# One-hots of the expert gates: 16-bit operands on VectorE, tokens innermost, eight at a step, in a hybrid decoder step

## The chip, the cores and the metric

The kernel runs on one core of a Trainium2 chip. The metric is the device time of one execution in microseconds (us). Before the change three runs took 4259.34, 4259.7 and 4266.0 us; the median is 4259.7. Lines (L974) are lines of the kernel before.

## The reference

One layer of a decoder trunk on 544 tokens (512 of a prompt, 8 sequences of 4 sampled ones), width 2048, everything in float32. A recurrence branch and a sliding-window attention branch are merged by sigmoid gates; then comes a product-key expert mixer (PEER), then a per-layer input embedding. The change is in the mixer:

```python
q = (xt @ w_q).reshape(n, PEER_HEADS, 2, D_KEY // 2)          # 8 heads, two halves of 128
s = jnp.einsum('nhpd,hpkd->nhpk', q, sub_keys)                # 128 keys each
s1, i1 = lax.top_k(s[:, :, 0], 16); s2, i2 = lax.top_k(s[:, :, 1], 16)
cand = s1[..., :, None] + s2[..., None, :]; cidx = i1[..., :, None] * 128 + i2[..., None, :]
top_s, sel = lax.top_k(cand.reshape(n, 8, 256), 16)           # 16 picks a head
idx = jnp.take_along_axis(cidx.reshape(n, 8, 256), sel, axis=-1); g = jax.nn.softmax(top_s, axis=-1)
hb = jax.nn.gelu(jnp.einsum('chkd,cd->chk', u[idx], x))       # 16384 experts
out = jnp.einsum('chk,chkd->cd', hb * g, v[idx])
```

So every token has 128 picks (8 heads by 16), each a pair of key indices (a, b), which name expert 128 a + b, and a gate.

## The kernel before, in words

**Dense and fetched tokens.** The first 416 tokens (`DC`) meet all 16384 experts in two dense products: H = gelu(U x) in 128 output tiles, then V^T (H * G), where G holds each token's gates at its experts and zero elsewhere. The last 128 tokens fetch their experts' rows of U and V one by one with indirect DMAs that GpSimd issues (L1039). A fetched row of U is multiplied with the tokens on VectorE (L1046); a fetched row of V is scaled on ScalarE (L1052) and added up on GpSimd (L1053).

**The weight pipeline.** All products run through `run_units`. A unit is a half chunk of 8 tiles of 128x128 weights. SyncE loads it (`wr`, L217), ScalarE rounds it to the high half (`wh`, L224), VectorE subtracts to get the low half (`wl`, L225), three buffers each, and the split of a unit is issued two units ahead. Every weight tile then makes three matmuls (high by high, high by low, low by high). In the products with U and V these are matmuls of 416 columns at L280, 24 a unit. An output tile of U is two units; VectorE scales its sum (L1092), ScalarE applies gelu (L1093) and issues the write to DRAM (L1094).

**The order of the side work.** Everything else that belongs beside the products is written as generators. Each `yield` names a cost in us of VectorE (0.5 where it names none). `side()` is called twice a unit, after four matmuls and at the unit's end. It adds a credit (1.256 in the product with U), takes off what a use of a fetched U row costs (2.3), and runs steps (`advance`) until the credit is used. So the order of instructions on every engine's queue is fixed when the program is built; only the waits are decided at run time. Before the 24th unit from the end of U (`gates_done`), all steps that are still open are run at once.

**The gates.** The generators run one after another. For each tile of 128 tokens (the last has 32) `tk1` and `tk2` find the picks on VectorE (top 16, index arithmetic) and bring them to `pt`, one pick on each partition and the tokens along the row: a, b and gate. Then G is made. For each token, a one-hot of a (128 picks by 128 keys) and a one-hot of b times the gate, multiplied on TensorE, give the 128x128 square of gates of that token. The gate stands as a sum of two float16 numbers (a high and a low part, `gh`), so each square is two matmuls that add up.

- L997 and L999 make, for four tokens, the one-hots `ob` and `oa` on VectorE: `iota` (float32) is compared with b or a (float32), with a float16 output, keys innermost, 128x512 elements.
- L1001 multiplies the one-hot of b with the low and the high part of the gates on GpSimd, twice 128x512.
- `place` (L974) takes the oldest of up to `QB` = 4 held groups: 8 matmuls of 128 columns into a PSUM tile `aux` (two buffers, of which one half is used). One step later ScalarE copies it to `gst` (L976) with the tokens innermost, so that it writes every 128 bytes.
- After 32 tokens (`TC`) ScalarE issues the write of `gst` (one buffer, 2 MB) to `Gd` in DRAM (L978). The product with V reads it back later.

The 416 tokens make 104 groups of four, 832 matmuls and 13 writes.

Of the kernel before, what the change touches and what calls it, by code (L numbers as in the profile page):

```python
# [9 lines left out]
F32 = mybir.dt.float32  # L10
# [7 lines left out]
P = 128  # L18
D = 2048
KT = D // P  # L20
NP = 512            # prompt tokens
NB, ND = 8, 4       # sample batch, tokens per sequence
T = NP + NB * ND    # token columns: prompt, then (b, t)
HB = T // 2
LP = 568            # columns of the recurrence layout: prompt, 3 spare, then (b, 7)
LH = LP // 2
RN = 8              # recurrence tiles
EPS = 1e-6
NEG = -1e30
NS = P              # last token columns, whose experts' rows are fetched one by one  # L30
DC = T - NS         # token columns that meet all experts in dense products
TC = 32             # tokens per chunk of the gate scratch
NCH = DC // TC
NW = 24             # operand pairs of the second PEER product
QB = 4
# [7 lines left out]
NWA = 2 * KT * T // (2 * DC)    # of these, the pairs that lie in the activations' space  # L43


def _token_tiles(t0, t1):
    """Tiles of nt tokens with ng head groups on the partitions: row = group * nt + token."""
    out = []
    while t0 < t1:
        nt = next(n for n in (128, 64, 32) if n <= t1 - t0)  # L50
        out.append((t0, nt, P // nt))
        t0 += nt
    return out
# [13 lines left out]
def _build(ctx, tc, nc, I, O):  # L67
# [47 lines left out]
    # sum of squares of the raw columns, folded to 1/rms of every column on every partition  # L115
    ssum = {}

    def sq_add(k, pool, x=0):
        """x: whose sum it joins, VectorE's or GpSimd's (which squares for itself)"""
        new = x not in ssum  # L120
        if new:
            ssum[x] = misc[:, (4 + x) * T:(5 + x) * T]
        s = ssum[x] if new else pool.tile([P, T], F32, name="sq", tag=f"sq{x}", bufs=2 - x)
        if x:
            GP.tensor_mul(s, raw[:, k, :], raw[:, k, :])
        else:
            A.activation(s, raw[:, k, :], AF.Square)
        if not new:
            (GP if x else V).tensor_add(ssum[x], ssum[x], s)
# [18 lines left out]
    def side():  # L148
        """A part of the work beside the products: steps worth pace["main"] us of the vector engine."""
        SPS["tick"] = SPS.get("tick", 0) + 1  # L150
        owed["sp"] += pace["sp"]
        if owed["sp"] >= 1:
            owed["sp"] -= 1
            owed["main"] -= sp_step()
        owed["main"] = min(owed["main"] + pace["main"], 2 * pace["main"])
        while owed["main"] > 0:
            c, more = advance()
            owed["main"] -= c
            if not more:
                break  # L160
# [4 lines left out]
    def unit(src, groups, **kw):  # L165
        """src: [128, 8, 128]; groups: (accumulator key, [(kl, operand getter)], start, stop, epilogue)"""
        units.append(dict(src=src, groups=groups, **kw))

    def gemm(src, ops, epi, nk=2, cols=None, **kw):
        """One output tile: nk half chunks of 8 k tiles, operands ops(k)."""  # L170
# [8 lines left out]
    def advance():  # L179
        cost, more = 0.0, bool(active or gens)  # L180
        while len(active) < maxact[0] and gens:
            if gens[0] is None:      # what follows needs everything before it
# [148 lines left out]
    # RG-LRU branch  # L331
# [10 lines left out]
    def decay_rate():  # L342
        # sp4 = 4 * softplus(-lam), with log1p kept accurate for small arguments
# [97 lines left out]
    # attention branch  # L441
# [208 lines left out]
    def start_ple():  # L650
        for k in range(2):
            t = pL.tile([P, T], F32, name="pin", tag="pin", bufs=2)
            SP.dma_start(out=t, in_=I["pT"][k])
            h, l = act_tile(KT - 2 + k)      # free until the last operands of w_in are split
# [95 lines left out]
    NGB = 3             # buffers of fetched rows  # L750
# [27 lines left out]
    def post_out():  # L778
# [4 lines left out]
        U_["iota"] = aconst(pU, "iota", [P, P])  # L783
# [3 lines left out]
    def rs_and_x():  # L787
        yield from make_rs(rs2)
        xg = U_["p"].tile([P, KT, NS], F32, name="xg", tag="gst", bufs=1)
# [37 lines left out]
    def scores(q):  # L827
        pU = U_["p"]
        kt = pU.tile([P, 4, P], F32, name="skl", tag="eq", bufs=1)
        SP.dma_start(out=kt, in_=I["skT"][:, q * 4:q * 4 + 4, :])  # L830
        for ti, (t0, nt, ng) in enumerate(TT):
# [7 lines left out]
            st = pU.tile([P, 512], F32, name="scst", tag="scst", bufs=2)  # L839
# [13 lines left out]
    def tk1(ti, q):  # L853
# [5 lines left out]
        sc = pU.tile([P, 4, P], F32, name="scp", tag="scp", bufs=2)  # L859
# [11 lines left out]
        # pairs (a, b) of ranks with (a + 1)(b + 1) <= 16 hold the 16 best: a = 0, then 1..7 with b < 8,  # L871
        # then 8..15 with b = 0, in the order of the flat index
# [13 lines left out]
    def tk2(ti):  # L886
# [5 lines left out]
        # ranks (a, b) of every pick, from its place among the pairs  # L892
# [18 lines left out]
        # the chosen key pair of every pick  # L911
        for x in range(2):
            for h2 in range(0, nh, 2):
# [3 lines left out]
                eq = pU.tile([P, 2, 16, 16], F32, name="eq", tag="eq", bufs=1)  # L917
                V.tensor_tensor(out=eq[:, :w], in0=U_["iota"][:, None, None, 0:16].to_broadcast(sh),
# [7 lines left out]
        # gates  # L926
# [20 lines left out]
        for x in range(3):  # L947
# [3 lines left out]
            # rows (group, token) to rows (group, pick): every group's picks in columns of its own  # L951
            ex = pU.tile([P, ng, n], F32, name="ex", tag="ex", bufs=2)
# [9 lines left out]
        # a gate, times GS to keep it in float16's range, as the sum of two float16  # L962
        g16 = pU.tile([P, P], F16, name="g16", tag="mk", bufs=1)
        gh = pU.tile([P, 2, P], F32, name="gh", tag="hu", bufs=1)
        A.activation(g16[:, :nt], pt[:, 2, :nt], AF.Copy, scale=GS)
        A.activation(gh[:, 0, :nt], g16[:, :nt], AF.Copy)
        yield
        V.scalar_tensor_tensor(gh[:, 1, :nt], pt[:, 2, :nt], GS, gh[:, 0, :nt], op0=ALU.mult, op1=ALU.subtract)
        def place(c0, gst, q0, oa, ob):
            ps = psum.tile([P, 2, 512], F32, name="aux", tag="aux", bufs=2)  # L970
            pq = ps[:, 0, :].rearrange("p (q i) -> p q i", i=P)
            for q in range(4):
                for x in range(2):
                    PE.matmul(pq[:, q], lhsT=oa[:, q, :], rhs=ob[:, q, x, :], start=x == 0, stop=x == 1)  # L974
            yield
            A.activation(gst[:, :, q0:q0 + 4].rearrange("p i q -> p q i"), pq, AF.Copy, scale=1.0 / GS)  # L976
            if q0 == TC - 4:
# [5 lines left out]
        def place_next():  # L983
            c0, q0, oa, ob = held.popleft()
# [4 lines left out]
            yield from place(c0, gst[0], q0, oa, ob)  # L989

        for c0 in range(0, nt, TC):
            for q0 in range(0, TC, 4):
                oa = pU.tile([P, 4, P], F16, name="oa", tag="oa", bufs=QB)
                ob = pU.tile([P, 4, 2, P], F16, name="ob", tag="ob", bufs=QB)
                tk = slice(c0 + q0, c0 + q0 + 4)
                io = U_["iota"][:, None, :].to_broadcast([P, 4, P])
                V.tensor_tensor(out=ob[:, :, 0, :], in0=io, in1=pt[:, 1, tk, None].to_broadcast([P, 4, P]),  # L997
                                op=ALU.is_equal)
                V.tensor_tensor(out=oa, in0=io, in1=pt[:, 0, tk, None].to_broadcast([P, 4, P]), op=ALU.is_equal)  # L999
                for x in (1, 0):  # L1000
                    GP.tensor_tensor(out=ob[:, :, x, :], in0=ob[:, :, 0, :],  # L1001
                                     in1=gh[:, x, tk, None].to_broadcast([P, 4, P]), op=ALU.mult)
                yield 1.2
                held.append((c0, q0, oa, ob))
# [6 lines left out]
    # the fetched experts: one pick of every row of a sparse tile at a time, the rows of U against the  # L1011
    # tokens on the vector engine, those of V, a batch later, into the sums on GpSimd
# [136 lines left out]
    def wfirst():  # L1149
        """Products for the first group; the operands that fit beside U's."""  # L1150
# [18 lines left out]
    def wsecond():  # L1169
        """In place of the first half of U's operands."""  # L1170
# [32 lines left out]
    def weave(n=3):  # L1203
        """The first halves of the last n tiles, then the second halves."""
# [34 lines left out]
    # operands of the last product go where the last group's W leave room, in the order that they leave  # L1239
# [28 lines left out]
    def post_first(g, lo, hi):  # L1268
        """The first halves of the last tiles are through: their operands' place is free."""
# [179 lines left out]
```

## Time and profile before

| | |
|---|---|
| median of three runs | 4259.7 us |
| profiled execution, span | 4266.4 us |
| TensorE (PE) busy | 4122.2 us, 97% |
| weight loads (PEld) busy | 4024.8 us, 94% |
| VectorE (DVE) busy | 2807.7 us, 66% |
| ScalarE (ACT) busy | 1534.6 us, 36% |
| GpSimd (POOL) busy | 1224.6 us, 29% |
| product with U, about | 1520 to 2900 us |
| product with V, about | 2900 to 4040 us |

The profiled execution is one execution recorded by the hardware, and its own time is the span: 4266.4 us from the first to the last record, 6.7 us above the median of the runs. Busy time is the union of an engine's instructions. [...] A view of waits names, for an engine's line, the instruction whose end it waited for. A view of stretches gives the busy time of each engine within given bounds. Views by form keep groups of instructions of the same shapes apart, with busy time, the mean of one in ns, and the engine's idle time before them with what ended it.

### The profile page before, as it was taken

Reading aid. Unit: us, or ns where it says so; the run is one execution under the profiler, and the core shown is the slowest. Engines: PE = TensorE matmul, PEld = TensorE weight load, DVE = VectorE, ACT = ScalarE, POOL = GpSimd, SP = SyncE. Lnnn points to the kernel's source line nnn. Section 1 sums busy time; section 2 is a strip of 40 time slices with the busy share of each in tenths; the row PEclk is TensorE's granted clock in tenths of the full one; section 3 lists DMA queues with packets and bytes.
Section 4 is the critical chain, followed back from the end, with each engine's and each line's share of the span. In section 5 each row is a group of like instructions: output and inputs, shape, how many; then the busy total and the mean of one; then the engine's idle time right before and its main releaser. Section 6 shows DMA issues by size and latency. Waiting matters only on the chain.

```text
span 4266.4 us, 63247 instructions
## 1 busy us (share of the span) xinstructions
PE 4122.2 (97%) x26089; PEld 4024.8 (94%) x26089; DVE 2807.7 (66%) x3659; ACT 1534.6 (36%) x1799; POOL 1224.6 (29%) x723
## 2 busy tenths in 40 slices
PE   7999999999999999999888988889999999999999
PEld 7999999999999999999878988889999999999999
DVE  7755444233434369888887988757888878877443
ACT  4442334321223233343343344334444444332331
POOL 3000000000000001464485377413555555410000
PEclk9999999999999999999999999999999999999999
DMA  5232232243343347677666666668989888997333
GB/s 180 80 125 79 75 106 86 84 135 134 124 131 104 111 144 266 234 274 254 215 231 213 233 209 217 224 221 289 332 312 332 326 315 314 323 327 248 118 131 102
DMA packets 323154, 848.69 MB, mean 199 GB/s; under 512 B 26409, under 2 KB 170729, under 8 KB 290097
## 3 DMA queue, kind: packets, MB, share of 16 engines
q1 hardware_dynamic: 204960, 492.69, 34.3%
q0 software_dynamic: 44864, 295.20, 18.6%
q10 hardware_dynamic: 73040, 56.76, 4.0%
q8 instruction: 204, 3.34, 0.3%
q14 instruction: 86, 0.70, 0.0%
HBM read 760.78 MB, written 83.77 MB: 198 GB/s over the span
## 4 chain that ended last, share of the span: by engine, by line
PE 85%; DVE 9%; ACT 2%; issue 2%; DMA 1%; ACTq 1%; POOL 0%; SPq 0%; DVEq 0%
PE acc L280 45%; PE acc L284 36%; DVE wl L225 4%; DVE raw L1046 1%; PE aux L974 1%; ACTq L1094 1%; ACT wh L224 1%; DVE misc L1092 1%; PE aux L519 1%; ACT gst L976 1%; PE aux L556 1%; DMA Gd<-gst 0%; PE aux L284 0%; ACT misc L1093 0%; PE aux L836 0%
## 5 line engine op out<-in xcount | busy, mean ns | idle before, releaser
L225 DVE TENSOR_TENSOR wl<-wr,wh 128x1024 fp32r<-128x1024 f32 x764 | 1220.6, 1599 | 1291.3 <-ACT wh L224 1287.7
L280 PE MATMUL acc<-opf,wh 128*128 128x416 f32 x7424 | 2038.5, 356 | 0.9 <-ACT wh L224 0.9
L280 PEld LDWEIGHTS acc<-opf,wh 128*128 128x128 f32 x7424 | 1405.4, 191 | 16.5 <-ACT wh L224 1.8
L224 ACT ACTIVATE wh<-wr 128x1024 fp32r<-128x1024 f32 x764 | 805.0, 1058 | 1577.9 <-PE acc L284 801.3
L284 PE MATMUL acc<-opf,wh 128*128 128x272 f32 x7936 | 1348.9, 292 | 22.3 <-ACT wh L224 9.1
L280 PE MATMUL acc<-opf,wl 128*128 128x416 f32 x3712 | 1316.5, 355 | 52.1 <-DVE wl L225 52.0
L284 PEld LDWEIGHTS acc<-opf,wh 128*128 128x128 f32 x7936 | 1140.7, 190 | 36.0 <-issue 15.1
L284 PE MATMUL acc<-opf,wl 128*128 128x272 f32 x3968 | 827.7, 290 | 0.0
L280 PEld LDWEIGHTS acc<-opf,wl 128*128 128x128 f32 x3712 | 708.8, 191 | 68.4 <-DVE wl L225 62.8
L284 PEld LDWEIGHTS acc<-opf,wl 128*128 128x128 f32 x3968 | 628.5, 189 | 0.3 <-DVE wl L225 0.3
L1001 POOL TENSOR_TENSOR ob<-ob,gh 128x512 f16<-128x512 f16 x208 | 313.1, 1510 | 71.2 <-DVE ob L997 60.1
L1053 POOL TENSOR_TENSOR raw<-raw,gb 128x2048 f32<-128x2048 f32 x59 | 276.8, 4692 | 124.2 <-ACT gb L1052 123.9
L1093 ACT ACTIVATE misc<-misc 128x416 f32<-128x416 f32 x128 | 70.6, 552 | 573.1 <-DVE misc L1092 573.1
L1039 POOL DMA_INDIRECT gb<-i_vn,idx x91 | 115.9, 1274 | 384.2 <-DVE gb L1046 222.5
L1053 POOL TENSOR_TENSOR raw<-raw 128x2048 f32<-128x2048 f32 x37 | 177.8, 4805 | 161.6 <-ACT raw L1052 161.6
L280 PE MATMUL acc<-wx,wh 128*128 128x416 f32 x768 | 206.8, 350 | 0.0
L1046 DVE SCALAR_TENSOR_TENSOR raw<-raw,misc 128x2048 f32<-128x2048 f32 x69 | 172.8, 2504 | 0.0
L1039 POOL DMA_INDIRECT raw<-i_un,idx x69 | 104.7, 1517 | 231.7 <-DVE raw L1046 153.5
L644 POOL DMA_DIRECT2D sg<-sgt x32 | 17.4, 543 | 510.3 <-ACT sgt L643 510.3
L280 PEld LDWEIGHTS acc<-wx,wh 128*128 128x128 f32 x768 | 143.8, 187 | 1.4
L1046 DVE SCALAR_TENSOR_TENSOR gb<-gb,misc 128x2048 f32<-128x2048 f32 x59 | 134.4, 2279 | 0.0
L280 PE MATMUL acc<-wx,wl 128*128 128x416 f32 x384 | 134.2, 349 | 0.0
(299 smaller groups left out, 2915.2 us busy)
## 6 DMA issues: line engine op xcount, KB each, us to landing
wr<-i_u SPq DMA_DIRECT2D x256, 512.0 KB
wr<-i_v SPq DMA_DIRECT2D x256, 512.0 KB
wr<-i_w_in SPq DMA_DIRECT2D x120, 512.0 KB
Hd<-misc ACTq DMA_DIRECT2D x128, 208.0 KB
Gd<-gst ACTq DMA_DIRECT2D x13, 2048.0 KB
gt<-Gd SPq DMA_DIRECT2D x32, 832.0 KB
misc<-Hd SPq DMA_DIRECT2D x112, 208.0 KB
wr<-i_w_proj SPq DMA_DIRECT2D x32, 512.0 KB
```

The costliest lines, as they stand in the source:

```text
L224: A.activation(hit[u], r, AF.Copy)
L225: V.tensor_sub(lot[u], r, hit[u].bitcast(F32))
L280: PE.matmul(acc[:, 0, :ncol], lhsT=w[:, kl, :], rhs=x[:, :ncol], start=st and t == 0, stop=sp and t == 2)
L284: PE.matmul(acc[:, s, :HB], lhsT=w[:, kl, :], rhs=x[:, s * HB:(s + 1) * HB], start=st and t == 0, stop=sp and t == 2)
L519: PE.matmul(sc[:, g, j0:], lhsT=raw[hs, RN + 4 * kp + g, blk * P:(blk + 1) * P], rhs=Q["k", kp][hs, ks:ks + nk], start=True, stop=True)
L556: PE.matmul(ps[hs, 0, :], lhsT=Q["v", kp][:, blk - 1 + kb, hs], rhs=pt[:, kb, :], start=kb == kbs[0], stop=kb == 1)
L974: PE.matmul(pq[:, q], lhsT=oa[:, q, :], rhs=ob[:, q, x, :], start=x == 0, stop=x == 1)
L1001: GP.tensor_tensor(out=ob[:, :, x, :], in0=ob[:, :, 0, :], in1=gh[:, x, tk, None].to_broadcast([P, 4, P]), op=ALU.mult)
L1039: GP.indirect_dma_start(out=t, out_offset=None, in_=I[kind + "n"], in_offset=bass.IndirectOffsetOnAxis(ap=idx[:, i:i + 1], axis=0))
L1046: V.scalar_tensor_tensor(t, t, 1.0, xtok, op0=ALU.mult, op1=ALU.mult, accum_out=hsp[:, i:i + 1])
L1053: GP.tensor_add(vacc, vacc, t)
L1093: A.activation(h, h, AF.Gelu_apprx_tanh)
```

## The change

The one-hots of a and b are made by one VectorE operation for eight tokens, in float16 throughout, with the tokens innermost (`oo`, 2 x 128 keys x 8 tokens). For this, the key numbers are laid out once, each eight times over (`irep`), and a and b are cast to float16 (`px`). A second VectorE operation multiplies the one-hot of b with both parts of the gate (`gl`); GpSimd's products are gone. `place` handles eight tokens in two steps of 8 matmuls, whose operands now step over 8 elements, and fills both halves of the PSUM tile. One evacuation writes eight tokens. `QB` is 2 groups of eight. Some buffers are shared or resized. Comments are removed too.

```diff
-QB = 4
+QB = 2
+QT = 8
...
-        U_["iota"] = aconst(pU, "iota", [P, P])
+        io = pU.tile([P, 512], F32, name="io", tag="scp", bufs=3)
+        SP.dma_start(out=io[:, :P], in_=I["iota"])
+        U_["iota"] = pU.tile([P, 16], F32, name="iota")
+        U_["irep"] = pU.tile([P, P, QT], F16, name="irep")
+        U_["io"] = io
...
         yield from make_rs(rs2)
+        V.tensor_copy(U_["iota"], U_["io"][:, :16])
+        V.tensor_copy(U_["irep"], U_["io"][:, :P, None].to_broadcast([P, P, QT]))
...
-        kt = pU.tile([P, 4, P], F32, name="skl", tag="eq", bufs=1)
+        kt = pU.tile([P, 4, P], F32, name="skl", tag="eq", bufs=2)
...
-            st = pU.tile([P, 512], F32, name="scst", tag="scst", bufs=2)
+            st = pU.tile([P, 512], F32, name="scst", tag="scp", bufs=3)
...
-        sc = pU.tile([P, 4, P], F32, name="scp", tag="scp", bufs=2)
+        sc = pU.tile([P, 4, P], F32, name="scp", tag="scp", bufs=3)
...
-            ex = pU.tile([P, ng, n], F32, name="ex", tag="ex", bufs=2)
+            ex = pU.tile([P, ng, n], F32, name="ex", tag="ex", bufs=1)
...
-        g16 = pU.tile([P, P], F16, name="g16", tag="mk", bufs=1)
-        gh = pU.tile([P, 2, P], F32, name="gh", tag="hu", bufs=1)
-        A.activation(g16[:, :nt], pt[:, 2, :nt], AF.Copy, scale=GS)
-        A.activation(gh[:, 0, :nt], g16[:, :nt], AF.Copy)
+        px = pU.tile([P, 2, P], F16, name="px", tag="mk", bufs=1)
+        g16 = pU.tile([P, 2, P], F16, name="g16", tag="hu", bufs=1)
+        A.activation(px[:, :, :nt], pt[:, 0:2, :nt], AF.Copy)
+        A.activation(g16[:, 0, :nt], pt[:, 2, :nt], AF.Copy, scale=GS)
         yield
-        V.scalar_tensor_tensor(gh[:, 1, :nt], pt[:, 2, :nt], GS, gh[:, 0, :nt], op0=ALU.mult, op1=ALU.subtract)
-        def place(c0, gst, q0, oa, ob):
+        V.scalar_tensor_tensor(g16[:, 1, :nt], pt[:, 2, :nt], GS, g16[:, 0, :nt], op0=ALU.mult, op1=ALU.subtract)
+        def place(c0, gst, q0, oo, gl):
             ps = psum.tile([P, 2, 512], F32, name="aux", tag="aux", bufs=2)
-            pq = ps[:, 0, :].rearrange("p (q i) -> p q i", i=P)
-            for q in range(4):
+            pq = ps.rearrange("p s (q i) -> p (s q) i", i=P)
+            for q in range(QT):
                 for x in range(2):
-                    PE.matmul(pq[:, q], lhsT=oa[:, q, :], rhs=ob[:, q, x, :], start=x == 0, stop=x == 1)
-            yield
-            A.activation(gst[:, :, q0:q0 + 4].rearrange("p i q -> p q i"), pq, AF.Copy, scale=1.0 / GS)
-            if q0 == TC - 4:
+                    PE.matmul(pq[:, q], lhsT=oo[:, 0, :, q], rhs=gl[:, x, :, q], start=x == 0, stop=x == 1)
+                if q == QT // 2 - 1:
+                    yield
+            yield
+            A.activation(gst[:, :, q0:q0 + QT], pq.rearrange("p q i -> p i q"), AF.Copy, scale=1.0 / GS)
+            if q0 == TC - QT:
...
-            for q0 in range(0, TC, 4):
-                oa = pU.tile([P, 4, P], F16, name="oa", tag="oa", bufs=QB)
-                ob = pU.tile([P, 4, 2, P], F16, name="ob", tag="ob", bufs=QB)
-                tk = slice(c0 + q0, c0 + q0 + 4)
-                io = U_["iota"][:, None, :].to_broadcast([P, 4, P])
-                V.tensor_tensor(out=ob[:, :, 0, :], in0=io, in1=pt[:, 1, tk, None].to_broadcast([P, 4, P]),
-                                op=ALU.is_equal)
-                V.tensor_tensor(out=oa, in0=io, in1=pt[:, 0, tk, None].to_broadcast([P, 4, P]), op=ALU.is_equal)
-                for x in (1, 0):
-                    GP.tensor_tensor(out=ob[:, :, x, :], in0=ob[:, :, 0, :],
-                                     in1=gh[:, x, tk, None].to_broadcast([P, 4, P]), op=ALU.mult)
+            for q0 in range(0, TC, QT):
+                oo = pU.tile([P, 2, P, QT], F16, name="oo", tag="eq", bufs=2)
+                gl = pU.tile([P, 2, P, QT], F16, name="gl", tag="gl", bufs=QB)
+                tk = slice(c0 + q0, c0 + q0 + QT)
+                sh = [P, 2, P, QT]
+                V.tensor_tensor(out=oo, in0=U_["irep"][:, None].to_broadcast(sh),
+                                in1=px[:, :, None, tk].to_broadcast(sh), op=ALU.is_equal)
                 yield 1.2
-                held.append((c0, q0, oa, ob))
+                V.tensor_tensor(out=gl, in0=oo[:, 1:2].to_broadcast(sh), in1=g16[:, :, None, tk].to_broadcast(sh),
+                                op=ALU.mult)
+                yield 1.2
+                held.append((c0, q0, oo, gl))
```

## Rows read from the trace of the kernel before

**Rows 1.** Waits of TensorE, 1700-2850 us: line, waited for: us, times, longest.
```profile
PE aux L974 <- ACT gst L976: 51.4, 18, 5.4
PE acc L280 <- DVE wl L225: 49.5, 24, 4.5
PE aux L974 <- POOL ob L1001: 7.8, 5, 2.9
```

**Rows 2.** Stretches: bounds, length, busy us (instructions) by engine, PEclk, DMA share, GB/s.
```profile
core 0: us, PE busy (x) PEld busy (x) DVE busy (x) ACT busy (x) POOL busy (x), PEclk, DMA share, GB/s
1545.00:1745.00 200.00, 200.00 (x1074) 199.26 (x1073) 175.11 (x425) 65.31 (x76) 26.89 (x19) 1.00 0.67 235
1745.00:1900.00 155.00, 152.31 (x918) 146.83 (x917) 131.93 (x126) 61.98 (x68) 98.98 (x64) 0.99 0.74 255
1900.00:2110.00 210.00, 198.31 (x1078) 190.98 (x1077) 181.35 (x348) 81.72 (x86) 90.09 (x43) 0.98 0.69 241
2110.00:2300.00 190.00, 161.72 (x941) 151.56 (x940) 159.81 (x121) 77.39 (x79) 149.25 (x83) 0.93 0.63 216
2300.00:2420.00 120.00, 107.33 (x545) 104.67 (x546) 100.89 (x271) 44.74 (x44) 47.23 (x20) 0.91 0.65 226
2420.00:2610.00 190.00, 163.21 (x930) 155.15 (x929) 162.14 (x135) 79.10 (x82) 126.82 (x70) 0.94 0.64 220
2610.00:2900.00 290.00, 259.77 (x1386) 249.46 (x1385) 192.73 (x243) 111.40 (x125) 110.61 (x59) 0.93 0.65 217
```

**Rows 3.** The same view, line 280 alone (PE, PEld), and a stretch of the V product.
```profile
1745.00:1900.00 155.00, 146.03 (x742) 137.88 (x741) 0.99 0.74 255
1900.00:2110.00 210.00, 195.37 (x995) 186.54 (x994) 0.98 0.69 241
2110.00:2300.00 190.00, 151.67 (x709) 138.78 (x708) 0.93 0.63 216
2300.00:2420.00 120.00, 105.99 (x521) 103.13 (x522) 0.91 0.65 226
2420.00:2610.00 190.00, 155.40 (x759) 145.28 (x758) 0.94 0.64 220
2610.00:2900.00 290.00, 249.64 (x1228) 238.79 (x1227) 0.93 0.65 217
2900.00:3200.00 300.00, 300.00 (x1592) 297.18 (x1591) 1.00 0.88 319
```

**Rows 4.** Timeline of TensorE around one `place`: start, duration, what.
```profile
2144.05 0.62 PE L974 MATMUL aux<-ob,oa 128*128 128x128 f16 x8
2144.48 0.62 PE L280 MATMUL acc<-opf,wh 128*128 128x416 f32 x2
```

**Rows 5.** Groups by form, 2110-2300 us: busy us, mean ns, idle before.
```profile
L1001 POOL TENSOR_TENSOR ob<-ob,gh 128x512 f16<-128x512 f16 x62 | 93.3, 1510 | 21.1 <-DVE ob L997 18.5
L225 DVE TENSOR_TENSOR wl<-wr,wh 128x1024 fp32r<-128x1024 f32 x31 | 72.9, 2355 | 30.2 <-ACT wh L224 30.2
L997 DVE TENSOR_TENSOR ob<-iota,pkT 128x512 f16<-128x512 f32 x30 | 39.1, 1302 | 0.0
L976 ACT ACTIVATE gst<-aux 128x512 f32<-128x512 f32 x27 | 28.8, 1092 | 7.2 <-DMA Gd<-gst 3.9 <-ACT misc L1093 3.2
L999 DVE TENSOR_TENSOR oa<-iota,pkT 128x512 f16<-128x512 f32 x30 | 28.0, 933 | 0.0
```

**Rows 6.** Groups by form, 900-1500 us.
```profile
L225 DVE TENSOR_TENSOR wl<-wr,wh 128x1024 fp32r<-128x1024 f32 x95 | 116.1, 1225 | 348.0 <-ACT wh L224 348.0
```

**Rows 7.** Stretches, line 225 alone (DVE busy).
```profile
2300.00:2420.00 120.00, 38.91 (x21) 0.91 0.65 226
```

**Rows 8.** Groups by form, 3500-4266 us, VectorE on 2048 elements; the reduction reads every 512 bytes.
```profile
L1055 DVE SCALAR_TENSOR_TENSOR raw<-gb,hsp,raw 128x2048 f32<-128x2048 f32 x32 | 75.0, 2343 | 0.0
L1087 DVE TENSOR_REDUCE gb<-gb 128x128 f32<-128x2048 f32 x1 | 3.9, 3873 | 2.0 <-ACT gb L1084 2.0
```

**Rows 9.** Groups by form, 900-1500 us: an evacuation that writes packed.
```profile
L840 ACT ACTIVATE scst<-aux 128x512 f32<-128x512 f32 x12 | 7.2, 598 | 20.1 <-PE aux L836 19.4
```

**Rows 10.** Timeline of ScalarE: a DMA issue behind a write of `gst`.
```profile
2272.59 5.37 ACTq L1094 DMA_DIRECT2D Hd<-misc  x1
```

More of the change, by code (lines that the diff above doesn't have):

```diff
@@ L916, in tk2 @@
                 sh = [P, w, 16, 16]
-                eq = pU.tile([P, 2, 16, 16], F32, name="eq", tag="eq", bufs=1)
-                V.tensor_tensor(out=eq[:, :w], in0=U_["iota"][:, None, None, 0:16].to_broadcast(sh),
+                eq = pU.tile([P, 2, 16, 16], F32, name="eq", tag="eq", bufs=2)
+                V.tensor_tensor(out=eq[:, :w], in0=U_["iota"][:, None, None, :].to_broadcast(sh),
                                 in1=hf[:, x, ss].rearrange("p (h j) -> p h j", h=w)[:, :, :, None].to_broadcast(sh),
@@ L983, in place_next @@
         def place_next():
-            c0, q0, oa, ob = held.popleft()
+            c0, q0, oo, gl = held.popleft()
             if q0 == 0:
@@ L988, in place_next @@
                 gst[0] = pU.tile([P, P, TC], F32, name="gst", tag="gst", bufs=1)
-            yield from place(c0, gst[0], q0, oa, ob)
+            yield from place(c0, gst[0], q0, oo, gl)
         for c0 in range(0, nt, TC):
-            for q0 in range(0, TC, 4):
-                oa = pU.tile([P, 4, P], F16, name="oa", tag="oa", bufs=QB)
-                ob = pU.tile([P, 4, 2, P], F16, name="ob", tag="ob", bufs=QB)
-                tk = slice(c0 + q0, c0 + q0 + 4)
-                io = U_["iota"][:, None, :].to_broadcast([P, 4, P])
-                V.tensor_tensor(out=ob[:, :, 0, :], in0=io, in1=pt[:, 1, tk, None].to_broadcast([P, 4, P]),
-                                op=ALU.is_equal)
-                V.tensor_tensor(out=oa, in0=io, in1=pt[:, 0, tk, None].to_broadcast([P, 4, P]), op=ALU.is_equal)
-                for x in (1, 0):
-                    GP.tensor_tensor(out=ob[:, :, x, :], in0=ob[:, :, 0, :],
-                                     in1=gh[:, x, tk, None].to_broadcast([P, 4, P]), op=ALU.mult)
+            for q0 in range(0, TC, QT):
[5 more added lines that the diff above has]
+                                in1=px[:, :, None, tk].to_broadcast(sh), op=ALU.is_equal)
                 yield 1.2
-                held.append((c0, q0, oa, ob))
+                V.tensor_tensor(out=gl, in0=oo[:, 1:2].to_broadcast(sh), in1=g16[:, :, None, tk].to_broadcast(sh),
+                                op=ALU.mult)
+                yield 1.2
+                held.append((c0, q0, oo, gl))
                 if len(held) == QB:
```

## The prediction, made before the changed kernel was run

> **What bounds the kernel now.** I read the share of busy time first: TensorE 97%, so at most a few per cent are to be had, and only where TensorE waits. The waits of TensorE say where: between 1700 and 2850 us it waited 51.4 us for the evacuations of the gate squares (`gst`), 49.5 us for the low halves of the weights (`wl`), 7.8 us for GpSimd's products (`ob`) [rows 1]. That stretch is the product with U, beside which the gates are made. The table of stretches shows the same: TensorE is full in 1545-1745, where VectorE is busy for 175.1 of 200 us with top-16 work, and again after 2900; between, in 2110-2300, it is busy 161.72 of 190 us at a granted clock of 0.93 [rows 2]. So VectorE at 88% does not stop TensorE by itself.
>
> How much is lost: one unit of the product is 24 matmuls of line 280. In 2900-3200 these follow each other without a gap, 1592 in 300 us, 4.523 us a unit [rows 3]. Eight matmuls of `place` hold TensorE for 0.43 us, from their first start to the next matmul's [rows 4]. The count of line 280 in each stretch [rows 3], and the matmuls besides it (all TensorE's less line 280's, by eights) [rows 2, 3], give the time that TensorE needs; the rest is lost to waits and to the lower clock after them:
> 1745-1900: 742, 22 places, needs 149.3 of 155, lost 5.7.
> 1900-2110: 995, 10 places, 191.8 of 210, lost 18.2.
> 2110-2300: 709, 29 places, 146.1 of 190, lost 43.9.
> 2300-2420: 521, 3 places, 99.5 of 120, lost 20.5.
> 2420-2610: 759, 21 places, 152.0 of 190, lost 38.0.
> 2610-2900: 1228, 19 places, 239.6 of 290, lost 50.4.
> Together 176.7 us. Nothing outside these stretches is touched, so this is the ceiling.
>
> **Why it is lost.** The steps beside the products are paced by fixed credits. A pair of one-hots counts 1.2 us, yet in 2110-2300 the two cost 1.302 + 0.933 = 2.24 us, and the split of a weight chunk 2.355 us [rows 5], where it is 1.225 us with GpSimd quiet [rows 6]. VectorE's operations there lengthen while GpSimd multiplies 62 times for 1510 ns. VectorE falls behind, ScalarE waits in its own order for VectorE's epilogue (L1092, L1093) before it comes to the evacuation, and `place`, with two `aux` buffers, waits for the evacuation two places back.
>
> **The change, part by part.**
> GpSimd: the 208 products go (313 us of its time by 208 x 1.51 [rows 5]). GpSimd's row fetches and sums of V rows, queued behind them, come earlier; its time is not on the path except through VectorE.
>
> VectorE: 104 pairs go, 52 pairs of operations on 2048 elements come (`oo`, `gl`). None such is in the trace. Upper end: three-operand work on 2048 float32, 2.343 us [rows 8]. Lower end: the new operand, 2048 elements of 2 bytes, has the bytes of the 1024 float32 of a weight split, 1.225 us [rows 6]; below that it can hardly go, since it would move more bytes per ns than any two-source row here. I take 1.225: all three operands become 16 bits wide with 8 neighbours innermost, which the old ones (float32 in) were not. Both new steps count 1.2, so credit and cost agree.
>
> In 2110-2300: 30 pairs took 39.1 + 28.0 = 67.1 us; for the same tokens 15 new pairs take 15 x 2.45 = 37, and I leave 7 us for waits behind the seven sums on GpSimd that stay: -23. The 31 splits go from 2.355 to what they cost where there are sums but few products, 38.91/21 = 1.85 us [rows 7]: -15. VectorE falls from 159.8 to about 122 us in the 146 that TensorE needs, 83%; less than the 88% that it carries unharmed in 1545-1745 [rows 2]. I count 85% of the loss as regained there and in 2420-2610, which has the same mix: 37 + 32. I keep 15% for bursts and for ScalarE's stalls at a DMA issue behind the 2 MB write of a gate chunk (5.37 us in one [rows 10]), which stay 13 in number.
> In 1900-2110 and 2300-2420 VectorE is taken by the top-16, whose steps cost more than their credit: 181.4 us for 191.8 and 100.9 for 99.5 [rows 2]. The change does not touch that; I count 6 + 6 us for entering without arrears. 1745-1900: 3.
> 2610-2900 holds the last 19 places and the point where all steps still open are run at once; TensorE waits for GpSimd's products there (most of the 7.8 us [rows 1]). The new step list is shorter by 4 credits (per tile, a tail of one held step instead of three), so less is left over, and the products are gone: 26 of 50.4.
> Sum: 3 + 6 + 37 + 6 + 32 + 26 = 110 us.
>
> PSUM: two places now hold 16 tokens instead of 8, so between an evacuation and the place that needs its buffer lie 5.8 credits instead of 2.9; that is where the 51.4 us go. What is late next is `wl` behind the top-16.
>
> ScalarE: 104 evacuations of 512 become 52 of 1024. Ends: twice the old 1.092 us [rows 5], and somewhat below one unstrided evacuation doubled, 2 x 0.598 [rows 9]; either way no more time than now, so nothing is counted.
>
> Small parts: the copy into `irep` and that into `iota` are two operations before the first tile's work, on a VectorE that idles between splits in that stage (348 us before 95 splits [rows 6]): zero, about 2 us without that cover. `ex` with one buffer makes three small matmuls of the last tile alternate with VectorE: 2 us. `scp` and the score stage share three buffers: zero, or some 4 us if an evacuation waits for a top-16. 110 - 2 = 108.
>
> TensorE: 832 place matmuls stay, but both operands now step over 8 elements, 16 bytes, from column to column. This price lies on the path in full. The trace has no strided operand of TensorE. Lower end: zero, since no column can come sooner than when packed. Upper end: strided work on other engines, taken as an absolute rate: VectorE's reduction with a step of 512 bytes takes 3.873 us for 2048 elements, about 1.85 ns each [rows 8]; 8 x 128 x 1.85 = 1.89 us instead of 0.43, times 104 = +152. Between them the ratio of those rows: 3.873/2.343 = 1.65, and an evacuation that writes at a step of 128 bytes against one that doesn't, 1.092/0.598 = 1.83 [rows 5, 8, 9]. The ratio is nearest, as TensorE runs its own pace: 0.43 x 0.74 x 104 = +33.
> [...]
>
> Net 108 - 33 = 75. The profiled execution has a span of 4266.4 us, 6.7 above the median of the runs, 4259.7; the same 75 off the median gives 4185 us.
>
> **The rivals.**
> 1. Slower: TensorE's strided columns cost the absolute rate, +152. Then `place` is itself the bound: 108 - 152 = -44, some 15 of it hidden, as VectorE's arrears in the top-16 stretches are then smaller: about 4290. For: the fastest packed stream into TensorE here is 1.81 ns for each 16 bytes (1592 matmuls of 416 4-byte columns in 300 us [rows 3]), and VectorE's strided read needs 1.85 ns for each element. Against: those steps are 128 and 512 bytes, not 16. It decides from 1.47 us per eight matmuls (0.43 + 108/104). [...] Chance 0.24.
> 2. The new VectorE operations run at float32's rate, 2.343 us: 15 pairs cost 70 us, as much as now; only the splits' 15 us and the drain are won, and the stride is partly hidden behind VectorE: about 4230. For: no two-source row here is faster than about 1 ns an element. [...] Chance 0.12.
> 3. The loss stays where it is: VectorE's freed time is not what held TensorE, but the top-16 steps and ScalarE's DMA issues; half the gain, 54, less 33: about 4240, down to nothing. For: 38.7 of 176.7 us lie in top-16 stretches, and VectorE is idle 30.2 us for ScalarE in 2110-2300 [rows 5]. Against: the places carry the 51.4 us. Chance 0.16.
>
> **How the numbers follow.** Forecast 0.48, with its own range from 4145 (no stride price, all of the places' loss regained) to 4220. The range 4145 to 4288 takes in rivals 2 and 3 and about half of rival 1. The measurement tells 0.2%, 8.5 us, from no change. Faster: 0.48 + 0.12 x 0.7 + 0.16 x 0.6 = 0.66; within: 0.12 x 0.2 + 0.16 x 0.3 + 0.24 x 0.1 = 0.10; slower 0.24.
>
> **What would show it.** `oo` and `gl` at about 1.2 us, 104 of them; no products on GpSimd; splits under 1.9 us in the place stretches; TensorE's wait for `gst` under 15 us; eight place matmuls between 0.43 and 0.9 us; a granted clock of 0.97 or more in 2100-2600. Wrong if eight place matmuls take 1.5 us or more, if `oo` takes 2.3 us, or if the time lost beside the top-16 grows.

## The result, and the profile after

The changed kernel takes 4297.5 us (median of 4 runs) against 4261.4 us of the kernel before beside it: ratio 1.0077, 95% interval 1.0063 to 1.0091. It is 0.8% slower. The forecast was 4185 us: the measured time lies outside the stated range (4145 to 4288) and on the other side of no change. Rival 1 (`place` itself the bound, about 4290 us) is what happened. In the kernel after, line numbers are up to 9 higher: the product is L281, `place` L982.

What TensorE waited for, 1500 to 3000 us (line, waited for: us, times, longest):

```profile
PE acc L281 <- DVE wl L226: 27.6, 14, 5.1
PE aux L963 <- DVE ex L962: 7.9, 3, 5.4
PE acc L281 <- ACT wh L225: 1.9, 2, 1.0
```

Against [rows 1] (its three sums are the same for 1500 to 3000 us) the wait for `gst` (51.4 us) and that for GpSimd's products (7.8) are gone, and the wait for the splits is down from 49.5. So the waits that the change aimed at did go. The groups by form in 1700-2930 us, the whole stretch of places (busy us, mean ns, idle before), first before, then after:

```profile
L225 DVE TENSOR_TENSOR wl<-wr,wh 128x1024 fp32r<-128x1024 f32 x223 | 430.9, 1936 | 230.0 <-ACT wh L224 229.6
L1001 POOL TENSOR_TENSOR ob<-ob,gh 128x512 f16<-128x512 f16 x208 | 313.1, 1510 | 71.2 <-DVE ob L997 60.1 <-ACT wh L224 2.4
L997 DVE TENSOR_TENSOR ob<-iota,pkT 128x512 f16<-128x512 f32 x104 | 113.7, 1093 | 0.0
L999 DVE TENSOR_TENSOR oa<-iota,pkT 128x512 f16<-128x512 f32 x104 | 102.8, 988 | 0.0
```

```profile
L226 DVE TENSOR_TENSOR wl<-wr,wh 128x1024 fp32r<-128x1024 f32 x217 | 340.3, 1569 | 352.6 <-ACT wh L225 352.2
L982 PE MATMUL aux<-gl,oo 128*128 128x128 f16 x832 | 213.2, 413 | 0.0
L1010 DVE TENSOR_TENSOR gl<-oo,g 128x2048 f16<-128x2048 f16 x52 | 76.6, 1472 | 1.5
L1007 DVE TENSOR_TENSOR oo<-irep,px 128x2048 f16<-128x2048 f16 x52 | 66.0, 1269 | 40.2 <-PE aux L982 40.2
L986 ACT ACTIVATE gst<-aux 128x1024 f32<-128x1024 f32 x52 | 53.3, 1025 | 94.9 <-PE aux L982 80.1 <-DMA Gd<-gst 8.5 <-ACT misc L1102 5.7
```

VectorE's new operations are as fast as hoped (medians of 1218 and 1225 ns), the splits take 1569 ns on average instead of 1936, and now VectorE (40.2 us) and ScalarE (80.1 us) wait for `place`, not the other way round. The timeline of TensorE around one `place` shows why, beside [rows 4], whose next line stands last here:

```profile
1801.78 2.05 PE L982 MATMUL aux<-gl,oo 128*128 128x128 f16 x8
1803.47 0.74 PE L281 MATMUL acc<-opf,wh 128*128 128x416 f32 x2
1804.04 0.35 PE L281 MATMUL acc<-opf,wl 128*128 128x416 f32 x1
```

```profile
2144.94 0.35 PE L280 MATMUL acc<-opf,wl 128*128 128x416 f32 x1
```

Eight matmuls hold TensorE for 1.69 us instead of 0.43, from their first start to the next matmul's. That count leaves most of the eighth to the product: inside a group the starts lie 232 ns apart (median over the trace; 56 ns before), and the two matmuls of the product behind it take 0.57 us (1803.47 to 1804.04) where they took 0.46 (2144.48 to 2144.94). With this tail a place costs 1.37 us more than before, not 1.26. The stretches of line 281 alone answer to [rows 3]:

```profile
1745.00:1900.00 155.00, 126.30 (x640) 119.53 (x638) 1.00 0.68 227
1900.00:2110.00 210.00, 183.37 (x933) 175.79 (x934) 0.99 0.66 225
2110.00:2300.00 190.00, 148.70 (x741) 138.61 (x741) 1.00 0.66 220
2300.00:2420.00 120.00, 104.73 (x525) 100.22 (x524) 0.97 0.66 231
2420.00:2610.00 190.00, 154.64 (x770) 146.01 (x768) 0.98 0.65 228
2610.00:2900.00 290.00, 239.90 (x1190) 229.03 (x1189) 0.96 0.63 216
```

The granted clock (PEclk, TensorE's as a share of its full speed) is back at 0.96 to 1.00 where it was 0.91 to 0.99. Yet in the same 1155 us TensorE did 4799 of these matmuls, 155 fewer than the 4954 before: 6.5 units, 29 us. Reckoned as in the prediction, 4799/24 x 4.523 = 904 us and 104 x 1.69 = 176 us are needed; 75 us are lost instead of 177. So 102 us came back, and 104 x 1.26 = 131 us went into `place`: 29 us worse, of the 32 between the two profiled spans (4298.4 and 4266.4 us). With the tail it is 104 x 1.37 = 142 us into `place` and 113 back; the difference stays.

### The profile page after: what moved, and what is told of

It reads as the page before. It is cut to its first block, busy times and chain, and to the rows that moved or that the text cites. A ratio compares the mean times of both kernels' runs of the same rounds, so it can differ in the third digit from the quotient of the medians.

```text
span 4298.4 us, 62653 instructions
## 1 busy us (share of the span) xinstructions
PE 4228.7 (98%) x26089; PEld 4078.9 (95%) x26089; DVE 2665.7 (62%) x3557; ACT 1490.7 (35%) x1747; POOL 893.2 (21%) x515
## 5 line engine op out<-in xcount | busy, mean ns | idle before, releaser
L281 PE MATMUL acc<-opf,wh 128*128 128x416 f32 x7424 | 2030.9, 355 | 1.9 <-ACT wh L225 1.9
L226 DVE TENSOR_TENSOR wl<-wr,wh 128x1024 fp32r<-128x1024 f32 x764 | 1135.4, 1487 | 1426.2 <-ACT wh L225 1424.4
L281 PEld LDWEIGHTS acc<-opf,wh 128*128 128x128 f32 x7424 | 1400.1, 189 | 26.8 <-ACT wh L225 2.4
L281 PE MATMUL acc<-opf,wl 128*128 128x416 f32 x3712 | 1303.7, 351 | 30.0 <-DVE wl L226 30.0
L281 PEld LDWEIGHTS acc<-opf,wl 128*128 128x128 f32 x3712 | 700.7, 189 | 42.3 <-DVE wl L226 37.5
L982 PE MATMUL aux<-gl,oo 128*128 128x128 f16 x832 | 213.2, 413 | 0.0
L281 PE MATMUL acc<-wx,wh 128*128 128x416 f32 x768 | 206.8, 350 | 0.0
L982 PEld LDWEIGHTS <-oo 128*128 128x128 f16 x832 | 112.2, 148 | 69.5 <-issue 19.0
L1055 DVE SCALAR_TENSOR_TENSOR raw<-raw,misc 128x2048 f32<-128x2048 f32 x69 | 157.5, 2283 | 0.0
L281 PEld LDWEIGHTS acc<-wx,wh 128*128 128x128 f32 x768 | 143.8, 187 | 1.4
L281 PE MATMUL acc<-wx,wl 128*128 128x416 f32 x384 | 134.3, 350 | 0.4 <-DVE wl L226 0.4
```

Source lines behind the costliest of these rows:

```text
L226: V.tensor_sub(lot[u], r, hit[u].bitcast(F32))
L281: PE.matmul(acc[:, 0, :ncol], lhsT=w[:, kl, :], rhs=x[:, :ncol], start=st and t == 0, stop=sp and t == 2)
L982: PE.matmul(pq[:, q], lhsT=oo[:, 0, :, q], rhs=gl[:, x, :, q], start=x == 0, stop=x == 1)
L1055: V.scalar_tensor_tensor(t, t, 1.0, xtok, op0=ALU.mult, op1=ALU.mult, accum_out=hsp[:, i:i + 1])
```

## The experiments

Each was timed beside the kernel before on the same chip. Ratios are to that kernel, with 95% intervals.

**packed: is it the step in place's operands?**

```diff
-PE.matmul(pq[:, q], lhsT=oo[:, 0, :, q], rhs=gl[:, x, :, q], ...)
+PE.matmul(pq[:, q], lhsT=oo[:, 0].rearrange("p k q -> p (k q)")[:, q * P:(q + 1) * P],
+          rhs=gl[:, x].rearrange("p k q -> p (k q)")[:, q * P:(q + 1) * P], ...)
```

> The changed kernel, but place reads both operands packed (128 columns next to each other, so the columns belong to the wrong keys and tokens; the pairing is left out). Theory A, the strided operands are the whole loss: eight place matmuls fall from the 1.68 us of the changed kernel to about 0.43, and 104 x 1.25 = 130 us go: about 4168 us, 2 to 2.5% faster than before the change. Theory B, the loss is in what VectorE or ScalarE now do (two-bank evacuation, waits of oo for place): eight place matmuls may shorten, but the time stays above 4250.

Measured: 4189.8 us, ratio 0.9822 (0.9806 to 0.9839). Timeline and waits of TensorE:

```profile
2108.16 0.62 PE L982 MATMUL aux<-gl,oo 128*128 128x128 f16 x8
2108.59 0.63 PE L281 MATMUL acc<-opf,wh 128*128 128x416 f32 x2
```

```profile
PE acc L281 <- DVE wl L226: 46.5, 23, 5.1
PE aux L963 <- DVE ex L962: 8.9, 3, 4.9
PE aux L982 <- DVE gl L1011: 4.0, 2, 2.2
```

Theory A holds: the eight matmuls are back at 0.43 us, and the kernel goes from 0.8% slower to 1.8% faster with nothing else changed. B is out. The time is 22 us above theory A's, and 19 of them show as waits: with `place` short TensorE waits 46.5 us for the splits, where it waited 27.6 in the changed kernel. Part of the 131 us had thus been hidden.

**wstep and mstep: which operand?** Each makes one of the two changes above: wstep packs the moving operand (`gl`) alone, mstep the weights (`oo`) alone.

> The changed kernel with only the weights of place (the one-hot of a) read at a step of 8 elements, the moving operand packed (wrong pairing, as in packed). Theory A1, the moving operand's reads are what is slow: near packed, eight matmuls at 0.45 to 0.6 us, about 4170 to 4185 us. Theory A2, the weight load is what is slow: eight matmuls at about 1.2 us or more (148 ns for each load in the changed kernel), 4250 us or more.

> The changed kernel with only the moving operand of place (gl) read at a step of 8 elements, the weights packed. Theory A1: eight matmuls stay at about 1.68 us and the time at about 4297 us. Theory A2: near packed, about 4170 us.

Measured: wstep 4191.8 us, ratio 0.9828 (0.9812 to 0.9845); mstep 4288.5 us, ratio 1.0056 (1.004 to 1.0073). Timelines of TensorE, wstep first:

```profile
2108.07 0.72 PE L982 MATMUL aux<-gl,oo 128*128 128x128 f16 x8
2108.59 0.63 PE L281 MATMUL acc<-opf,wh 128*128 128x416 f32 x2
```

```profile
1804.89 1.98 PE L982 MATMUL aux<-gl,oo 128*128 128x128 f16 x8
1806.51 0.74 PE L281 MATMUL acc<-opf,wh 128*128 128x416 f32 x2
```

With the weights at a step eight matmuls take 0.52 us, with the moving operand at a step 1.62. It is the moving operand (A1). Weights at a step of 16 bytes are nearly free (0.52 us against 0.43 packed).

**step4, step16 and pairs: the law of the price.** step4 and step16 read both operands with `[:, q:q + 4 * P:4]`, or at a step of 16 over the whole tile. pairs is a whole version with two tokens innermost (`irep` holds each key number twice):

```diff
+QR = 2
-oo = pU.tile([P, 2, P, QT], F16, name="oo", tag="eq", bufs=2)
+oo = pU.tile([P, 2, QT // QR, P, QR], F16, name="oo", tag="eq", bufs=2)
...
+for x in range(2):      # likewise for gl, with oo[:, 1], g16 and mult
+    V.tensor_tensor(out=oo[:, x], in0=U_["irep"][:, None].to_broadcast(sh), in1=tr(px[:, x, tk]), op=ALU.is_equal)
...
+PE.matmul(pq[:, q], lhsT=oo[:, 0, q // QR, :, q % QR], rhs=gl[:, x, q // QR, :, q % QR], ...)
```

> A whole version: two tokens innermost instead of eight (tiles of 4 groups x 128 keys x 2 tokens), so place steps over 2 elements, 4 bytes, and VectorE's four operations of 1024 elements per eight tokens stay in 16 bits. Theory L, an operand costs by the 16-byte lines that it touches, 1.64 ns each (1.68 us / 8 / 128): 32 lines are 52 ns a matmul, as packed: eight matmuls at about 0.43 to 0.5 us, VectorE's operations about 0.69 us each, and about 4165 to 4185 us. Theory S, any step but one element leaves the fast read: eight matmuls at about 1.7 us, about 4300 us.

> The changed kernel with both operands of place read at a step of 4 elements, 8 bytes, inside the same tiles (wrong pairing of keys and tokens). Theory L, the moving operand costs 1.64 ns for each 16-byte line: 64 lines, 105 ns a matmul, 0.84 us for eight instead of 0.43 packed and 1.68 at a step of 8: 104 x 0.41 = 43 us over packed, less what hides: about 4215 to 4235 us. Theory T, a threshold (8 bytes still free): 0.45 us, about 4190 us.

> The changed kernel with both operands of place read at a step of 16 elements, 32 bytes (wrong pairing). Theory L: one line a column as at a step of 8, so eight matmuls stay at 1.68 us and the time at about 4297 us. Theory D, the price grows with the distance: about 3.4 us for eight, 180 us more, about 4470 us.

Measured: pairs 4190.4 us, ratio 0.9819 (0.9803 to 0.9835); step4 4210.3 us, ratio 0.9863 (0.9846 to 0.9879); step16 4298.6 us, a single run. Timelines of TensorE in pairs, step4 and step16:

```profile
2105.58 0.64 PE L983 MATMUL aux<-gl,oo 128*128 128x128 f16 x8
2106.03 0.62 PE L282 MATMUL acc<-opf,wh 128*128 128x416 f32 x2
```

```profile
2120.84 1.11 PE L982 MATMUL aux<-gl,oo 128*128 128x128 f16 x8
2121.70 0.63 PE L281 MATMUL acc<-opf,wh 128*128 128x416 f32 x2
```

```profile
2201.78 2.08 PE L982 MATMUL aux<-gl,oo 128*128 128x128 f16 x8
2203.49 0.74 PE L281 MATMUL acc<-opf,wh 128*128 128x416 f32 x2
```

Eight matmuls take 0.43 us at a step of 1 element, 0.45 at 2, 0.86 at 4, 1.69 at 8 and 1.71 at 16. 128 columns touch 64, 128 and 128 lines of 16 bytes at steps 4, 8 and 16. Inside a group the starts lie 118, 232 and 234 ns apart (medians over the traces), which is 1.84, 1.81 and 1.83 ns for each line. (The times of eight give 1.65 to 1.68, as they leave out most of the eighth matmul.) At step 2 the 32 lines would need some 58 ns; the starts lie 60 ns apart, against 56 packed. Theory L fits all five steps, with a price some 10% above the 1.64 ns that it was written with; free reads at a step of 8 bytes (T) and a price by distance (D) are out. Steps that are no power of two, and operands of another type, were not tried. step4's total came out 5 us below what I expected; part hides here too, as TensorE waits 33.6 us for the splits, against 46.5 in packed. pairs keeps the whole gain of packed in a kernel that computes everything.

**gpload: was it GpSimd's load or VectorE's own one-hots?** pairs with GpSimd's old number of products, on a constant.

```diff
+GP.tensor_tensor(out=dead, in0=U_["irep"][:, None].to_broadcast([P, 2, P, QR]),
+                 in1=U_["irep"][:, None].to_broadcast([P, 2, P, QR]), op=ALU.mult)    # four for eight tokens
```

> The version with two tokens innermost, plus 208 GpSimd multiplications of 128x512 float16 on a constant into a tile that nobody reads (four for every eight tokens, as many as GpSimd had before). Theory C, GpSimd's products stretched VectorE's operations and this was most of the loss: the weight splits go from 1.68 us on average towards 1.99 and the time from 4190 to 4225 to 4250 us. Theory V, it was VectorE's own one-hots that were too slow: the time stays under 4200 us.

Measured: 4263.1 us, ratio 0.9988 (0.9978 to 0.9997). Groups by form in 1700-2930 us, first pairs, then gpload; behind them TensorE's waits, 1500 to 3000 us, in the same order:

```profile
L227 DVE TENSOR_TENSOR wl<-wr,wh 128x1024 fp32r<-128x1024 f32 x239 | 400.3, 1678 | 274.1 <-ACT wh L226 271.8 <-issue 2.0
L1015 DVE TENSOR_TENSOR gl<-oo,g 128x1024 f16<-128x1024 f16 x104 | 93.1, 936 | 1.5
L1011 DVE TENSOR_TENSOR oo<-irep,px 128x1024 f16<-128x1024 f16 x104 | 66.9, 684 | 3.0 <-PE aux L983 2.7
```

```profile
L227 DVE TENSOR_TENSOR wl<-wr,wh 128x1024 fp32r<-128x1024 f32 x223 | 406.2, 1828 | 175.8 <-ACT wh L226 175.5
L998 POOL TENSOR_TENSOR dead<-irep 128x512 f16<-128x512 f16 x208 | 287.3, 1381 | 13.7
L1024 DVE TENSOR_TENSOR gl<-oo,g 128x1024 f16<-128x1024 f16 x104 | 147.6, 1458 | 1.5
L1019 DVE TENSOR_TENSOR oo<-irep,px 128x1024 f16<-128x1024 f16 x104 | 130.4, 1293 | 0.0
```

```profile
PE acc L282 <- DVE wl L227: 43.6, 24, 4.2
```

```profile
PE acc L282 <- DVE wl L227: 87.7, 34, 7.5
PE aux L983 <- DVE gl L1024: 6.4, 5, 3.3
```

Products on GpSimd that nobody waits for lengthen `oo` from 684 to 1293 ns, `gl` from 936 to 1458 and the splits from 1678 to 1828, and take nearly the whole gain away: more than theory C had expected. With GpSimd multiplying beside it, VectorE's 16-bit version is worth next to nothing here (0.1%, where pairs gains 1.8%). The wait for `gst` does not come back, though VectorE is late again; the time is lost to the splits instead (87.7 us). The single operations show the same lengthening: in pairs the 205 splits of this stretch that overlap none of GpSimd's sums of V rows (L1066) take 1221 ns on average and at most 1228, the 34 that overlap one 4429 ns; the 97 `gl` clear of them take 687 ns, the other seven 4385.

**dve32: GpSimd's products moved, nothing else.** The kernel before, one word changed:

```diff
-GP.tensor_tensor(out=ob[:, :, x, :], in0=ob[:, :, 0, :], in1=gh[...], op=ALU.mult)
+V.tensor_tensor(out=ob[:, :, x, :], in0=ob[:, :, 0, :], in1=gh[...], op=ALU.mult)
```

> The kernel before with one line changed: the two products of the one-hot with the gate's parts run on VectorE instead of GpSimd, in the old layout (keys innermost, operands of place packed) and with float32 gates, so 416 operations of 128x512 on VectorE instead of 208. Theory C, taking GpSimd's load away is the gain, and VectorE's own time matters less: at 0.68 us each VectorE spends 283 us on one-hots against 216 stretched ones before, splits shorten to about 1.7 us: about 4225 to 4250 us, faster than before. Theory V, the 16-bit operations are needed for any gain: at or above 4265 us, with TensorE waiting more for the splits.

Measured: 4246.0 us, ratio 0.9944 (0.9927 to 0.9961). Groups by form (1700-2930 us), and TensorE's waits (1500 to 3000 us):

```profile
L225 DVE TENSOR_TENSOR wl<-wr,wh 128x1024 fp32r<-128x1024 f32 x226 | 374.0, 1658 | 199.6 <-ACT wh L224 199.3
L1001 DVE TENSOR_TENSOR ob<-ob,gh 128x512 f16<-128x512 f16 x208 | 169.2, 813 | 3.6
L999 DVE TENSOR_TENSOR oa<-iota,pkT 128x512 f16<-128x512 f32 x104 | 75.7, 728 | 0.0
L997 DVE TENSOR_TENSOR ob<-iota,pkT 128x512 f16<-128x512 f32 x104 | 75.6, 727 | 0.0
```

```profile
PE acc L280 <- DVE wl L225: 53.8, 30, 4.2
PE aux L974 <- ACT gst L976: 43.2, 20, 4.4
```

Doubling VectorE's one-hot operations made the kernel 0.6% faster, as theory C said: each is short again (727 ns against 1093 and 988 in the same stretch before), and so are the splits (1658 against 1936). VectorE then spends 320 us on them, against 160 in pairs. dve32 gains 22 us, pairs 75. The other 70% come with the 16-bit layout and with the places and evacuations of eight tokens, and only with GpSimd quiet. Which of these two gives how much is not shown: pairs has both and dve32 neither, and of dve32's waits 43.2 us are for `gst`.

**balanced: where is the rest?** pairs with other credits: `yield 1.0` to 1.6 and 1.1 to 1.5 in the top-16, 1.8 to 2.1 in the picks, 0.5 to 0.1 in `place`.

> The version with two tokens innermost, with credits nearer to what the steps cost VectorE: a top-16 step 1.6 instead of 1.0 and 1.5 instead of 1.1, a pick step 2.1 instead of 1.8, the steps of place 0.1 instead of 0.5. If what is left of the loss (TensorE waits 43.6 us for weight splits) comes from too much VectorE work a unit in the top-16 stretches, the waits fall below 25 us and the time to about 4165 to 4180. If it comes from GpSimd's sums and ScalarE's DMA issues, it stays within 10 us of 4190.

Measured: 4174.1 us, ratio 0.9782 (0.9765 to 0.9798). Waits of TensorE, 1500 to 3000 us:

```profile
PE acc L282 <- DVE wl L227: 32.8, 21, 4.1
PE aux L983 <- ACT gst L988: 11.7, 3, 4.3
PE aux L964 <- DVE ex L963: 8.6, 3, 6.4
```

16 us more, inside the expectation for the time, but the wait for the splits stays at 32.8 and not below 25 (43.6 in pairs), and 11.7 us of waits for `gst` come back, with the two steps of a place now mostly back to back. So uneven credits explain a part of what is left. For the rest the trace points at GpSimd's sums: here the 207 splits in 1700-2930 us that overlap none take 1221 ns on average, the 36 that do 4123, and about 20 of the 32.8 us of waits stand right behind such a split. No run leaves the sums out, so how much time they cost is not shown. This version beats both kernels, by 2.2% and 2.9%.

## Why the prediction was wrong

- **What bounds, and where the time is lost**: right. The loss of 177 us beside the U product, and the waits that carry it, are what the change moved.
- **VectorE's price**: right. 52 + 52 operations, medians 1218 and 1225 ns, where 1225 was taken. The means are 1269 and 1472, as five operations beside GpSimd's sums took 2530 to 5535 ns. The splits went to 1.57 us on average (1.85 taken). VectorE was busy for 120 us in 2110-2300 (122 forecast), though with about 24 places there instead of 29.
- **PSUM**: right. Twice the distance between an evacuation and its next user, and the 51.4 us went to zero. They stay at zero in gpload, where VectorE is late again, and at 43.2 us in dve32, which has the old places; that points at the places of eight tokens, though no run has them without the 16-bit operations.
- **The sum regained**: 108 forecast, 102 found in the changed kernel (113 with the tail of the eighth matmul). That this is near is luck. With `place` cheap (packed, pairs) it is only about 75: the 85% in the place stretches and the half of the end were too much. In the changed kernel the slow `place` itself gave VectorE time to catch up (27.6 us of waits for splits, 46.5 in packed).
- **Small parts**: `ex` cost 4.5 us instead of 2 (7.9 us of waits against the 3.4 us left out of [rows 1]). ScalarE as forecast, half its old time (53.3 us for the evacuations against 112.7 in 1700-2930 us).
- **The step that failed** is the price of TensorE's strided operands: "The ratio is nearest, as TensorE runs its own pace: 0.43 x 0.74 x 104 = +33". Measured: 1.26 x 104 = +131, and +142 with the tail of the eighth matmul. The two bounds were right (0 and +152); the choice between them was wrong, and the upper one was nearly the truth. I carried over how many times slower other engines get, when here their absolute time came much nearer: 1.85 ns for a strided element on VectorE [rows 8], 1.81 for each line on TensorE. Why the two are so near, no run shows. TensorE, at 0.42 ns for a packed 2-byte column, loses four times over by that (1.69 us against 0.43); VectorE, at 1.1 ns for an element, not even twice (3.873 us against 2.343 [rows 8]). The prediction had a further sign in hand, and named it under rival 1: TensorE's fastest packed stream, 1.81 ns for 16 bytes [rows 3], the very price of a line in the changed kernel.
- **Rival 1** was right in mechanism, place and point of decision (1.47 us for eight matmuls; it came to 1.69), and nearly in its time. It deserved more than 0.24. And the price does not begin at 16 bytes: at a step of 8 (step4), with two columns in every 16 bytes, a matmul already takes twice as long as packed (118 ns against 56).

## What to carry to other kernels

When a layout is turned to suit one engine, price it at every engine that reads it, in absolute time (here 1.81 ns for each 16 bytes that TensorE's moving operand touches), not as a ratio from another engine. For TensorE's moving operand in 2 bytes, two elements side by side were enough to stay nearly at the packed rate (0.45 against 0.43 us for eight matmuls), and VectorE's 16-bit operations were still fast on such pairs (684 ns for 1024, against 1221 for a float32 split of 1024). And where VectorE is late, look first at what GpSimd does beside it: moving GpSimd's products onto the late engine made the kernel 0.6% faster (dve32).

## What the hardware showed that was not expected

- Reading its operands at a step costs TensorE 1.81 to 1.84 ns for each 16-byte line of the moving operand once the columns lie 8 bytes or more apart, and hardly more at 32 bytes than at 16 (234 ns a matmul against 232). With the moving operand alone at 16 bytes (mstep) it is 1.78. The weights, at a step of 16 bytes, cost 0.09 us for eight loads.
- ScalarE reads PSUM at a step of 512 bytes at no cost that shows: the evacuation of 1024 elements takes 1025 ns with 8 columns written side by side, less than twice the 598 of a packed one of 512 [rows 9]. The old one of 512 took 1092 with a packed read and single elements written every 128 bytes [rows 5]. There the price was in the write.
- In gpload four idle-running GpSimd products for eight tokens nearly double a 16-bit operation of VectorE (684 to 1293 ns). In pairs a split either takes 1221 ns or, beside a GpSimd sum, 4429 on average: the mean of 1678 hides two kinds.
